# Attention: two-column minima and sums by one-source reductions instead of two-operand operations

## The chip, the cores and the metric

The kernel runs on one core of one Trainium2 chip. A core has TensorE (PE), VectorE (DVE), ScalarE (ACT), GpSimd (POOL) and a queue engine (SP), which run side by side and wait for each other by semaphores. The metric is the device time of one execution in microseconds, from the first to the last instruction of the program. Times are compared by the median of several executions.

## What is computed

A trunk of two layers over 1024 latent tokens and 256 context tokens in float32. The second layer's mixer is attention in two kinds of heads, 8 of each, with 64 columns: global heads that see all 1280 keys, and windowed heads that see the 256 context keys and three blocks of 128 latent keys and have one learned sink logit each. What matters here is the softmax:

```python
def attend(q, k, v, mask=None, sink=None):
    s = jnp.einsum('bqhgd,bkhd->bhgqk', q, k).astype(jnp.float32) * (HEAD_DIM ** -0.5)
    ...
    if sink is not None:
        col = jnp.broadcast_to(sink.astype(jnp.float32)[None, :, :, None, None], s.shape[:-1] + (1,))
        p = jax.nn.softmax(jnp.concatenate([s, col], axis=-1), axis=-1)[..., :-1]
    else:
        p = jax.nn.softmax(s, axis=-1)
    return jnp.einsum('bhgqk,bkhd->bqhgd', p.astype(v.dtype), v)
```

## The kernel before, in words

The attention is cut into 32 units: 2 kinds of heads, 2 groups of four heads, 8 blocks of 128 queries. The first 16 units are global (1280 keys, in ten blocks), the last 16 windowed with a sink (four or five blocks). The scores come negated, so that a row's greatest score is a minimum here, and the exponential is taken with a scale of −1.

For each head `h` of a unit `i`, TensorE writes the scores into PSUM: 1024 columns in `S` and 256 in `M` for a global head, one stretch of 512 or 640 columns in `S` for a windowed head (`do_chunk`, L2113). DVE takes the minimum of each part (`do_max`, L2119) into the tile `mx`, whose three rows of four columns hold the minimum of the first part, that of the second, and what is used. `do_bias` (L2125) takes the smaller of two columns: those of the two parts for a global head, that of the scores and the negated sink (`sinkn`) for a windowed head. ACT then takes the exponential with that column as its bias (`do_exp`, L2134) into `P` and adds up the row into a column of `rsum`, one for each part. In a windowed unit DVE adds the sink to the four minima (`do_arg`, L2140) and ACT takes the exponential of that as the second row of `rsum` (`do_sexp`).

After the four heads, TensorE transposes `P` by blocks of keys (`do_T`), ACT copies each block to `tf` (L2153), POOL rounds it to `th` (helper `rnd`, L73), and DVE, for the first block POOL, takes the rest `tl` = `tf` − `th` (helper `rest`, L77); TensorE multiplies `th` and `tl` with the values into `pv`. `do_recip` adds the two rows of `rsum` (L2179) and takes the reciprocal (L2180), POOL spreads it out to `R` (L2186), TensorE transposes it, ACT copies it. ACT copies parts of `pv` to `Yt` (L2206, L2207), DVE adds them into `Y` (L2213, L2214), POOL scales `Y` (L2219) and ACT and POOL split it into `ah` and `al`. In the first half, POOL also works on slices of the output weights (`woraw`, `woh`, `wol`, from `wo_steps`).

The order on all engines is made by a small planner at the end of `attention_units`: each step has an engine, a planned duration, a due time and the steps before it, and the steps are issued in the order in which the planner starts them. The planned durations are in the `op(...)` calls, and the engines carry their instructions out in that order.

Of the kernel before, what the change touches and what calls it, by code (L numbers as in the profile page):

```python
# [10 lines left out]
F32 = mybir.dt.float32  # L11
F32R = mybir.dt.float32r
AF = mybir.ActivationFunctionType
ALU = mybir.AluOpType
AX = mybir.AxisListType
# [22 lines left out]
def kernel(  # L38
# [6 lines left out]
    nc = tc.nc  # L45
    uid = [0]

    def nm(s):
        uid[0] += 1
        return f"{s}_{uid[0]}"  # L50
# [1994 lines left out]
    def attention_units(p, psS, psM, psT, psV, kv0, identr, bandr, sinkc, sinkn, wo_steps):  # L2045

        units = [(kind, g, qb) for kind in range(2) for g in range(2) for qb in range(8)]
# [3 lines left out]
        st, K, V = {}, {}, {}  # L2051
# [23 lines left out]
        def window(qb):  # L2075
            lo, hi = max(0, qb - 1), min(8, qb + 2)
            return 256 + lo * 128, (hi - lo) * 128
# [8 lines left out]
        def score_groups(i, h):  # L2086

            kind, g, qb = units[i]
            kh, kl = K[kind, g]
            q = st["q", i][:, h, :]  # L2090
            X = psS.tile([128, 1024], F32, tag="S", name=nm("S"))
            if not kind:
                M = psM.tile([128, 256], F32, tag="M", name=nm("M"))
                return ([(o, [(q, kh[:, k0:k0 + n]), (q, kl[:, k0:k0 + n])])
                         for o, k0, n in ((X[:, 0:512], 0, 512), (X[:, 512:1024], 512, 512), (M, 1024, 256))],
                        [X, M])
            k0, n = window(qb)
            b0 = 128 if qb == 0 else 0
            return ([(X[:, 256:512], [(q, kh[:, 0:256]), (q, kl[:, 0:256])]),
                     (X[:, 512:512 + n], [(q, kh[:, k0:k0 + n]), (identr, bandr[:, b0:b0 + n]), (q, kl[:, k0:k0 + n])])],  # L2100
                    [X[:, 256:512 + n]])

        def do_chunk(i, h, c):
            if c == 0:
                st["ch", i, h], st["sc", i, h] = score_groups(i, h)
            o, ops = st["ch", i, h][c]
            for x_, (l_, r_) in enumerate(ops):
                if l_ is identr and o.shape[1] == 384:

                    nc.tensor.matmul(o.rearrange("p (b k) -> p b k", k=128)[:, 0::2, :], lhsT=l_,  # L2110
                                     rhs=r_.rearrange("p (b k) -> p b k", k=128)[:, 0::2, :], start=False, stop=False)
                    continue
                nc.tensor.matmul(o, lhsT=l_, rhs=r_, start=x_ == 0, stop=x_ == len(ops) - 1)  # L2113


        def do_max(i, h, c):
            if h == 0 and c == 0:
                st["mx", i] = p.tile([128, 3, 4], F32, tag="mx", bufs=3, name=nm("mx"))
            nc.vector.tensor_reduce(out=st["mx", i][:, c, h:h + 1], in_=st["sc", i, h][c], axis=AX.X, op=ALU.min)  # L2119

        def do_bias(i, h):
            kind, g, qb = units[i]
            mx = st["mx", i]
            other = sinkn[:, 4 * g + h:4 * g + h + 1] if kind else mx[:, 1, h:h + 1]
            nc.vector.tensor_tensor(out=mx[:, 2, h:h + 1], in0=mx[:, 0, h:h + 1], in1=other, op=ALU.min)  # L2125

        def do_exp(i, h, c):
            if ("rs", i) not in st:
                st["rs", i] = p.tile([128, 2, 4], F32, tag="rsum", bufs=3, name=nm("rsum"))
            if ("P", i, h) not in st:  # L2130
                st["P", i, h] = p.tile([128, 1280], F32, tag=f"P{h}", bufs=2, name=nm("P"))
            rs, P, mx = st["rs", i], st["P", i, h], st["mx", i]
            o = st["sc", i, h][c]
            nc.scalar.activation(out=P[:, 1024 * c:1024 * c + o.shape[1]], in_=o, func=AF.Exp, scale=-1.0,  # L2134
                                 bias=mx[:, 2, h:h + 1], accum_out=rs[:, c, h:h + 1])
# [39 lines left out]

        def do_recip(i):
            rs3 = st.pop(("rs", i))
            rs = rs3[:, 0, :]
            nc.vector.tensor_tensor(out=rs, in0=rs, in1=rs3[:, 1, :], op=ALU.add)  # L2179
            nc.vector.reciprocal(out=rs, in_=rs)  # L2180
            st["rc", i] = rs

# [61 lines left out]
        for x_, (i, h) in enumerate(heads):  # L2244
            kind, n = units[i][0], nkb[i]
            t = starts[i] + h * (starts[i + 1] - starts[i]) / 4.0
            two = [("exp", *heads[x_ - 2], 0)] if x_ >= 2 else []
            one = [("exp", *heads[x_ - 1], 1)] if x_ >= 1 and not units[heads[x_ - 1][0]][0] else []
            width = 128 * (n - 2) + 256
            op(("chunk", i, h, 0), "PE", 0.215 if kind else 0.43, t, do_chunk, i, h, 0, deps=two)  # L2250
            op(("chunk", i, h, 1), "PE", (0.485 if n == 5 else 0.33) if kind else 0.43, t, do_chunk, i, h, 1,
               deps=[("chunk", i, h, 0)])
            if not kind:
                op(("chunk", i, h, 2), "PE", 0.215, t, do_chunk, i, h, 2, deps=[("chunk", i, h, 1)] + one)
            op(("max", i, h, 0), "DVE", 0.065 + width / 960.0 if kind else 1.131, t - 0.3, do_max, i, h, 0,
               deps=[("chunk", i, h, 1)])
            if not kind:
                op(("max", i, h, 1), "DVE", 0.333, t - 0.3, do_max, i, h, 1, deps=[("chunk", i, h, 2), ("max", i, h, 0)])
            op(("bias", i, h), "DVE", 0.075, t + 0.4, do_bias, i, h, deps=[("max", i, h, c) for c in range(2 - kind)])
            free_P = [("T", i - 2, nkb[i - 2] - 1)] if i >= 2 else []  # L2260
            op(("exp", i, h, 0), "ACT", 0.24 + width / 1200.0 if kind else 1.092, t + 2.7, do_exp, i, h, 0,
               deps=[("bias", i, h)] + free_P)
            if not kind:
                op(("exp", i, h, 1), "ACT", 0.452, t + 1.6, do_exp, i, h, 1, deps=[("bias", i, h)] + free_P)
# [18 lines left out]
            if kind:  # L2283
                op(("arg", i), "DVE", 0.08, T0, do_arg, i, deps=[("bias", i, h_) for h_ in range(4)])
                op(("sexp", i), "ACT", 0.19, T0 + 0.5, do_sexp, i, deps=[("arg", i)] + exps)
                exps.append(("sexp", i))
            op(("recip", i), "DVE", 0.30, T0 + 1.0, do_recip, i, deps=exps)
            op(("R", i), "Pool", 0.37, T0 + 1.0, do_R, i, deps=[("recip", i), ("RT", i - 1)])
            op(("RT", i), "PE", 0.22, T0 + 1.9, do_RT, i, deps=[("R", i), ("T", i, 0)], take="T")
# [55 lines left out]
        for x_, k in enumerate(order):  # L2345
            i = k[1]
# [483 lines left out]
```

## Time and profile before

| | us |
|---|---|
| median of three runs (2981.91 to 2985.57) | 2983.54 |
| the profiled execution | 2980.23 |
| its span from first to last instruction | 2978.5 |
| attention, global units (1786 to 2049 us of the span) | 263 |
| attention, windowed units (2049 to 2206 us) | 157 |
| TensorE busy over the span | 2793.1 (94%) |
| DVE busy over the span | 2138.9 (72%) |
| POOL busy over the span | 663.0 (22%) |

Busy shares over the whole span are means over stages that are limited by different engines; the edited lines run only in the attention, so its two halves are looked at by themselves. An operation's duration in the profile reaches from its start on the engine to its end and includes time in which it can't go on.

### The profile page before, as it was taken

The page shows a single profiled execution, that of the slowest core. Times are in us where ns is not written, and L with a number is a line of the kernel's source. Part 1 is how long each engine was busy: PE and PEld are TensorE (multiplying, and loading weights), DVE is VectorE, ACT ScalarE, POOL GpSimd, SP SyncE. Part 2 cuts the span into 40 slices and gives each one's busy share as a digit, 9 for nine tenths or more (in the row PEclk, how much of TensorE's full clock was granted, in tenths as well). Part 3 has the DMA queues.
Part 4 walks back from the last instruction along what each step waited for, and adds up shares of the span by engine and source line. Part 5 has one row for each costly group of instructions (what it writes and reads, how often), then busy time and mean ns, then how long its engine had stood idle before and what let it go on. Part 6 is the DMA issues. An engine that isn't in the chain of part 4 may idle for free. (4 is left out here: it accounts for less than half of the span.)

```text
span 2978.5 us, 37852 instructions
## 1 busy us (share of the span) xinstructions
PE 2793.1 (94%) x13912; PEld 2260.6 (76%) x13912; DVE 2138.9 (72%) x2995; ACT 1281.4 (43%) x2229; POOL 663.0 (22%) x729
## 2 busy tenths in 40 slices
PE   7999999887899999999999989998889899999997
PEld 4777767665688888888877876666768688888886
DVE  4898943545766666666776668999884877886778
ACT  2555531345322222234364527777764422222433
POOL 5223313111000000000024345777751000000002
PEclk9999999999899999999999999999999999999998
DMA  6344445665133355475675562102012343454854
GB/s 223 123 153 152 138 141 176 197 176 146 59 90 91 91 159 157 157 254 185 191 207 140 176 207 57 40 27 56 29 45 98 95 125 109 154 177 157 297 170 121
DMA packets 310809, 412.78 MB, mean 139 GB/s; under 512 B 19888, under 2 KB 188680, under 8 KB 305504
## 3 DMA queue, kind: packets, MB, share of 16 engines
q1 hardware_dynamic: 296608, 387.24, 41.0%
q0 software_dynamic: 8640, 15.79, 3.2%
q10 hardware_dynamic: 5376, 7.34, 0.7%
q8 instruction: 109, 1.79, 0.3%
q14 instruction: 76, 0.62, 0.1%
HBM read 311.85 MB, written 98.45 MB: 138 GB/s over the span
## 5 line engine op out<-in xcount | busy, mean ns | idle before, releaser
L80 PE MATMUL fi<-ah,sop 128*128 128x512 f32 (+1 forms) x1056 | 379.2, 359 | 16.3 <-ACT sop L69 13.3
L82 PE MATMUL fi<-ah,sop 128*128 128x512 f32 (+1 forms) x1056 | 377.6, 358 | 0.6 <-DVE sop L77 0.5
L81 PE MATMUL fi<-al,sop 128*128 128x512 f32 (+1 forms) x1056 | 377.8, 358 | 0.3 <-DVE al L77 0.3
L69 ACT CAST sop<-sraw 128x1024 fp32r<-128x1024 f32 (+1 forms) x198 | 176.5, 901 | 264.9 <-DVE sraw L1125 195.1
L77 DVE TENSOR_TENSOR sop<-sraw,sop 128x1024 fp32r<-128x1024 f32 (+1 forms) x198 | 203.8, 1047 | 93.6 <-ACT sop L69 93.6
L80 PEld LDWEIGHTS fi<-ah,sop 128*128 128x128 f32 x1056 | 202.7, 192 | 45.5 <-ACT sop L69 14.1
L82 PEld LDWEIGHTS fi<-ah,sop 128*128 128x128 f32 x1056 | 201.8, 191 | 30.9 <-DVE sop L77 2.6
L81 PEld LDWEIGHTS fi<-al,sop 128*128 128x128 f32 x1056 | 202.3, 192 | 28.7 <-DVE al L77 0.8
L80 PE MATMUL fi<-T,sop 128*128 128x512 f32 x528 | 206.6, 391 | 8.8 <-ACT T L69 7.2
L82 PE MATMUL fi<-T,sop 128*128 128x512 f32 x528 | 206.2, 391 | 0.5 <-DVE sop L77 0.5
L81 PE MATMUL fi<-T,sop 128*128 128x512 f32 x528 | 206.4, 391 | 0.0
L73 POOL TENSOR_SCALAR th<-tf 128x512 fp32r<-128x512 f32 x236 | 163.8, 706 | 97.6 <-ACT tf L2153 93.8
L77 DVE TENSOR_TENSOR tl<-tf,th 128x512 fp32r<-128x512 f32 x204 | 171.9, 857 | 13.1 <-POOL th L73 12.4
L80 PE MATMUL ip<-ah,whi 128*128 128x512 f32 (+1 forms) x480 | 175.6, 366 | 3.6 <-ACT ah L69 3.5
L81 PE MATMUL ip<-al,whi 128*128 128x512 f32 (+1 forms) x480 | 171.7, 358 | 0.5 <-DVE al L77 0.4
L82 PE MATMUL ip<-ah,wlo 128*128 128x512 f32 (+1 forms) x480 | 170.7, 356 | 0.0
L80 PE MATMUL fo<-fow,fos 128*128 128x512 f32 x385 | 150.6, 391 | 3.5 <-DVE acc L1128 2.2
L2153 ACT COPY tf<-T 128x512 f32<-128x512 f32 x236 | 133.3, 592 | 41.1 <-PE T L2148 25.5
L82 PE MATMUL fo<-fow,fos 128*128 128x512 f32 x385 | 150.0, 390 | 0.1
L81 PE MATMUL fo<-fow,fos 128*128 128x512 f32 x385 | 149.9, 389 | 0.0
L2148 PE MATMUL T<-ident,P 128*128 128x128 f32 x944 | 139.7, 274 | 1.4 <-ACT tf L2153 0.4
L2119 DVE TENSOR_REDUCE mx<-S 128x1 f32<-128x1024 f32 (+2 forms) x128 | 127.8, 999 | 14.2 <-PE S L2113 13.0
(413 smaller groups left out, 7092.5 us busy)
## 6 DMA issues: line engine op xcount, KB each, us to landing
sraw<-in_ffn_w_in_dram SPq DMA_DIRECT2D x88, 512.0 KB
adaraw<-in_ada_w_dram SPq DMA_DIRECT2D x40, 1024.0 KB
stream<-sd_d SPq DMA_DIRECT2D x77, 320.0 KB
stream<-in_ffn_w_out_dram SPq DMA_DIRECT2D x78, 256.0 KB
wt<-sd_d SPq DMA_DIRECT2D x77, 256.0 KB
sd_d<-hp SPq DMA_DIRECT2D x22, 640.0 KB
wt<-in_ffn_w_out_dram SPq DMA_DIRECT2D x55, 256.0 KB
h_d<-acc SPq DMA_DIRECT2D x26, 512.0 KB
```

The source lines that it names most:

```text
L69: nc.scalar.copy(out=o, in_=i)
L73: nc.gpsimd.tensor_scalar(out=o, in0=i, scalar1=1.0, scalar2=0.0, op0=ALU.mult, op1=ALU.add)
L77: e.tensor_tensor(out=o, in0=i, in1=hi.bitcast(F32), op=ALU.subtract)
L80: nc.tensor.matmul(ps, lhsT=sh, rhs=mh, start=start, stop=False)
L81: nc.tensor.matmul(ps, lhsT=sh, rhs=ml, start=False, stop=False)
L82: nc.tensor.matmul(ps, lhsT=sl, rhs=mh, start=False, stop=stop_)
L2119: nc.vector.tensor_reduce(out=st["mx", i][:, c, h:h + 1], in_=st["sc", i, h][c], axis=AX.X, op=ALU.min)
L2148: nc.tensor.transpose(ps_[:, x_ * 128:(x_ + 1) * 128], st["P", i, h][:, j * 128:(j + 1) * 128], ident)
L2153: nc.scalar.copy(out=tf, in_=st.pop(("T", i, j)))
```

## The change

The minimum of two columns and the sum of two rows, which were tensor_tensor operations, become tensor_reduce operations over an axis of two elements of one tile. For that, both values have to stand in one tile. In global units they do. In windowed units POOL first copies the four negated sinks of the group into the second row of `mx`, one new POOL operation a unit; so `mx` is taken in `do_chunk`, ahead of the unit's first scores, and no longer in `do_max`. `do_arg` later writes over that row, as before. `rsum` gets a third row for the sum, which was written in place.

```diff
--- before.py
+++ after.py
@@ -2103,6 +2103,12 @@
         def do_chunk(i, h, c):
             if c == 0:
                 st["ch", i, h], st["sc", i, h] = score_groups(i, h)
+            if h == 0 and c == 0:
+                st["mx", i] = p.tile([128, 3, 4], F32, tag="mx", bufs=3, name=nm("mx"))
+                kind, g = units[i][:2]
+                if kind:
+                    nc.gpsimd.tensor_scalar(out=st["mx", i][:, 1, :], in0=sinkn[:, 4 * g:4 * g + 4], scalar1=1.0, scalar2=0.0,
+                                            op0=ALU.mult, op1=ALU.add)
             o, ops = st["ch", i, h][c]
             for x_, (l_, r_) in enumerate(ops):
                 if l_ is identr and o.shape[1] == 384:
@@ -2114,19 +2120,15 @@
 
 
         def do_max(i, h, c):
-            if h == 0 and c == 0:
-                st["mx", i] = p.tile([128, 3, 4], F32, tag="mx", bufs=3, name=nm("mx"))
             nc.vector.tensor_reduce(out=st["mx", i][:, c, h:h + 1], in_=st["sc", i, h][c], axis=AX.X, op=ALU.min)
 
         def do_bias(i, h):
-            kind, g, qb = units[i]
             mx = st["mx", i]
-            other = sinkn[:, 4 * g + h:4 * g + h + 1] if kind else mx[:, 1, h:h + 1]
-            nc.vector.tensor_tensor(out=mx[:, 2, h:h + 1], in0=mx[:, 0, h:h + 1], in1=other, op=ALU.min)
+            nc.vector.tensor_reduce(out=mx[:, 2, h:h + 1], in_=mx[:, 0:2, h], axis=AX.X, op=ALU.min)
 
         def do_exp(i, h, c):
             if ("rs", i) not in st:
-                st["rs", i] = p.tile([128, 2, 4], F32, tag="rsum", bufs=3, name=nm("rsum"))
+                st["rs", i] = p.tile([128, 3, 4], F32, tag="rsum", bufs=3, name=nm("rsum"))
             if ("P", i, h) not in st:
                 st["P", i, h] = p.tile([128, 1280], F32, tag=f"P{h}", bufs=2, name=nm("P"))
             rs, P, mx = st["rs", i], st["P", i, h], st["mx", i]
@@ -2175,8 +2177,8 @@
 
         def do_recip(i):
             rs3 = st.pop(("rs", i))
-            rs = rs3[:, 0, :]
-            nc.vector.tensor_tensor(out=rs, in0=rs, in1=rs3[:, 1, :], op=ALU.add)
+            rs = rs3[:, 2, :]
+            nc.vector.tensor_reduce(out=rs, in_=rs3[:, 0:2, :].rearrange("p c h -> p h c"), axis=AX.X, op=ALU.add)
             nc.vector.reciprocal(out=rs, in_=rs)
             st["rc", i] = rs
 
```

On DVE a piece of a global unit's instructions stood so before the change (`mx` the minima, `tl` the rest of a block, `rsum` the row sums, `Y` the output of the unit before; the number behind a name tells buffers apart):

```order
L2119 TENSOR_REDUCE mx_15908<-M_15870 128x1
L2179 TENSOR_TENSOR rsum_15737<-rsum_15737 128x4
L2180 RECIPROCAL rsum_15737<-rsum_15737 128x4
L2125 TENSOR_TENSOR mx_15908<-mx_15908 128x1
L77 TENSOR_TENSOR tl_15948<-tf_15914,th_15929 128x512
L77 TENSOR_TENSOR tl_15957<-tf_15927,th_15936 128x512
L2119 TENSOR_REDUCE mx_15908<-S_15923 128x1
L2119 TENSOR_REDUCE mx_15908<-M_15924 128x1
L2125 TENSOR_TENSOR mx_15908<-mx_15908 128x1
L2213 TENSOR_TENSOR Y_16001<-pv_15807,Yt_15983 64x256
```

And so after it:

```order
L2123 TENSOR_REDUCE mx_15871<-M_15870 128x1
L2181 TENSOR_REDUCE rsum_15737<-rsum_15737 128x4
L2182 RECIPROCAL rsum_15737<-rsum_15737 128x4
L2127 TENSOR_REDUCE mx_15871<-mx_15871 128x1
L77 TENSOR_TENSOR tl_15948<-tf_15914,th_15929 128x512
L77 TENSOR_TENSOR tl_15957<-tf_15927,th_15936 128x512
L2123 TENSOR_REDUCE mx_15871<-S_15923 128x1
L2123 TENSOR_REDUCE mx_15871<-M_15924 128x1
L2127 TENSOR_REDUCE mx_15871<-mx_15871 128x1
L2215 TENSOR_TENSOR Y_16001<-pv_15807,Yt_15983 64x256
```

No instruction of DVE has moved; three lines of the piece have another operation and one source less. On PE, ACT and SP the order is the same too.

On POOL a piece of the windowed units stood so (`th` the rounded block, `al` the second part of the output's split, `R` the spread reciprocals):

```order
L73 TENSOR_SCALAR th_17908<-tf_17893 128x512
L77 TENSOR_TENSOR al_1842_13924<-Y_17865,ah_1841_13923 128x2x128
L2186 TENSOR_SCALAR R_17944<-rsum_17804 128x256
L73 TENSOR_SCALAR th_17971<-tf_17961 128x512
L2219 TENSOR_TENSOR Y_17963<-Y_17963,rT_17861 128x256
L77 TENSOR_TENSOR tl_17986<-tf_17961,th_17971 128x512
L73 TENSOR_SCALAR th_18008<-tf_17980 128x512
```

And after the change so:

```order
L73 TENSOR_SCALAR th_17915<-tf_17898 128x512
L77 TENSOR_TENSOR al_1842_13924<-Y_17870,ah_1841_13923 128x2x128
L2188 TENSOR_SCALAR R_17950<-rsum_17809 128x256
L73 TENSOR_SCALAR th_17977<-tf_17967 128x512
L2221 TENSOR_TENSOR Y_17969<-Y_17969,rT_17866 128x256
L77 TENSOR_TENSOR tl_17992<-tf_17967,th_17977 128x512
L2110 TENSOR_SCALAR mx_18009<-sinkn 128x4
L73 TENSOR_SCALAR th_18016<-tf_17986 128x512
```

The copy of the sinks (L2110) has been put between `tl` and `th`; there are 16 such copies, one a windowed unit, and nothing else on POOL has moved.

## Rows read from the trace of the kernel before

**Rows 1.** Windows: the two halves of the attention; busy us and instructions by engine, granted clock.

```profile
core 0: us, PE busy (x) PEld busy (x) DVE busy (x) ACT busy (x) POOL busy (x), PEclk, DMA share, GB/s
1786.00:2049.00 263.00, 238.50 (x1302) 177.52 (x1302) 245.37 (x385) 199.20 (x460) 179.46 (x224) 0.99 0.17 44
2049.00:2206.00 157.00, 139.35 (x848) 111.67 (x846) 143.00 (x276) 119.87 (x295) 111.49 (x147) 0.99 0.13 35
```

**Rows 2.** Chain that ended last, over 1870 to 1954 us: its shares by line.

```profile
by line: DVE tl L77 33.2%; DVE mx L2119 26.3%; DVE mx L2125 6.2%; POOL th L73 5.0%; PE T L2148 3.7%; PE S L2113 3.6%; issue 2.9%; PE pv L2174 2.8%; DVE Y L2214 2.0%; DVE Y L2213 1.9%; POOL wol L77 1.7%; PE pv L2173 1.7%; POOL woraw L2371 1.
```

**Rows 3.** Groups by line and form, DVE, 1786 to 2210 us (busy us, mean ns of one).

```profile
L77 DVE TENSOR_TENSOR tl<-tf,th 128x512 fp32r<-128x512 f32 x202 | 170.0, 855 | 13.1 <-POOL th L73 12.4
...
L2125 DVE TENSOR_TENSOR mx<-mx 128x1 f32<-128x1 f32 x64 | 28.3, 443 | 1.1
...
L2125 DVE TENSOR_TENSOR mx<-mx,sinkn 128x1 f32<-128x1 f32 x64 | 25.3, 396 | 0.8
...
L2179 DVE TENSOR_TENSOR rsum<-rsum 128x4 f32<-128x4 f32 x32 | 7.2, 225 | 0.0
...
L2140 DVE TENSOR_TENSOR mx<-mx,sinkc 128x4 f32<-128x4 f32 x16 | 7.2, 450 | 0.4
```

**Rows 4.** Line L2125: durations in ns (shortest, median, longest); who waited (us, times).

```profile
L2125 DVE TENSOR_TENSOR mx<-mx x64: 128/452/1232, 1786.6 to 2047.7; 128x1 f32<-128x1 f32 x64
...
L2125 DVE TENSOR_TENSOR mx<-mx,sinkn x64: 128/324/1244, 2049.4 to 2203.1; 128x1 f32<-128x1 f32 x64
...
  ACT P L2134: 45.1, 55
```

**Rows 5.** Timeline of DVE, 1943 to 1951.3 us (start us, duration us).

```profile
1943.78 0.56 DVE L2125 TENSOR_TENSOR mx<-mx 128x1 f32<-128x1 f32 x1
...
1944.26 0.68 DVE L77 TENSOR_TENSOR tl<-tf,th 128x512 fp32r<-128x512 f32 x1
...
1947.35 0.45 DVE L2125 TENSOR_TENSOR mx<-mx 128x1 f32<-128x1 f32 x1
...
1947.72 1.48 DVE L77 TENSOR_TENSOR tl<-tf,th 128x512 fp32r<-128x512 f32 x2
...
1950.70 0.56 DVE L2125 TENSOR_TENSOR mx<-mx 128x1 f32<-128x1 f32 x1
...
1951.27 0.42 DVE L2213 TENSOR_TENSOR Y<-pv,Yt 64x256 f32<-64x256 f32 x1
```

**Rows 6.** Timeline of POOL, 1943 to 1952 us.

```profile
1943.60 0.73 POOL L73 TENSOR_SCALAR th<-tf 128x512 fp32r<-128x512 f32 x1 [0.28 <-ACT tf L2153]
...
1946.60 1.20 POOL L73 TENSOR_SCALAR th<-tf 128x512 fp32r<-128x512 f32 x2 [2.26 <-ACT tf L2153]
...
1950.05 1.20 POOL L73 TENSOR_SCALAR th<-tf 128x512 fp32r<-128x512 f32 x2 [1.39 <-ACT tf L2153]
```

**Rows 7.** Groups by line and form, POOL, 1786 to 2210 us.

```profile
L2371 POOL TENSOR_TENSOR woraw<-woraw,wogate 128x512 f32<-128x512 f32 x6 | 9.5, 1579 | 0.0
```

**Rows 8.** DVE operations with one source in SBUF: shortest, median, longest in ns.

```profile
L2180 DVE RECIPROCAL rsum<-rsum x32: 177/178/180, 1796.7 to 2206.3; 128x4 f32<-128x4 f32 x32
...
L1866 DVE TENSOR_REDUCE ss<-t x13: 404/674/685, 1594.0 to 1742.9; 128x8 f32<-128x512 f32 x8, 128x4 f32<-128x256 f32 x5
```

**Rows 9.** Groups by form of line L1866 on DVE (busy us, mean ns of one).

```profile
L1866 DVE TENSOR_REDUCE ss<-t 128x8 f32<-128x512 f32 x8 | 5.4, 678 | 2.0 <-ACT t L1863 2.0
...
L1866 DVE TENSOR_REDUCE ss<-t 128x4 f32<-128x256 f32 x5 | 2.1, 413 | 1.6 <-ACT t L1863 1.6
```

**Rows 10.** Timeline of ACT, 1943.5 to 1951.9 us; idle time before in brackets.

```profile
1947.84 0.47 ACT L2134 ACTIVATE P<-M,mx 128x256 f32<-128x256 f32 x1 [0.84 <-DVE mx L2125]
...
1950.87 0.36 ACT L2207 COPY Yt<-pv 64x256 f32<-64x256 f32 x1
```

**Rows 11.** Timeline of DVE in the second half, 2110 to 2125 us.

```profile
2116.84 0.56 DVE L2125 TENSOR_TENSOR mx<-mx,sinkn 128x1 f32<-128x1 f32 x1
...
2118.08 0.82 DVE L2119 TENSOR_REDUCE mx<-S 128x1 f32<-128x640 f32 x1 [0.40 <-PE S L2113]
```

**Rows 12.** POOL tensor_scalar of line L129: shortest, median, longest in ns.

```profile
L129 POOL TENSOR_SCALAR rs<-mv x46: 212/222/1240, 442.7 to 2969.1; 128x1 f32<-128x1 f32 x46
```

## The prediction

> **What bounds the kernel now.** Read first the busy time of each engine over the attention, the only part in which the edited lines run. VectorE (DVE) is busy 245.4 of 263 us in the first half (the global heads) and 143.0 of 157 us in the second (the windowed heads with a sink), TensorE 238.5 and 139.4, GpSimd (POOL) 179.5 and 111.5 [rows 1]. Then the chain of work that ended last, over a stretch of the first half: the two largest entries are DVE's subtractions `tl` (L77, 33.2%) and its score minima (L2119, 26.3%), the third is L2125, one of the two edited lines, with 6.2% [rows 2]. So DVE sets the pace here. A one-column minimum has no business among the first three, which makes its duration the next thing to look at.
>
> L2125 takes one column from each of two sources, and yet its mean is 443 ns in the first half and 396 ns in the second [rows 3]; its shortest case is 128 ns, its longest 1244 [rows 4]. What fills the rest is seen in time. In one unit of the first half the minimum that starts at 1943.78 lasts 0.56 us, until 1944.34; POOL's rounding `th` that started at 1943.60 ends at 1944.33. The one at 1947.35 and the one at 1950.70 likewise end at 1947.80 and 1951.26, and POOL's pairs of `th` end at 1947.80 and 1951.25 [rows 5, 6]. An operation of DVE with two sources in SBUF thus waits until POOL's running operation is over. Operations of DVE with one source don't: RECIPROCAL on the same row sums has 177 to 180 ns in all 32 cases, and the tensor_reduce of L1866, which also reads float32 from SBUF, between 404 and 685 ns over its two widths, whose means are 413 and 678 ns [rows 8, 9].
>
> **The change part by part.** *Price of the new operation.* No row has a tensor_reduce over two columns. From the two widths of L1866, (678 − 413) / 256 = 1.04 ns a column, so a fixed part of 413 − 256 × 1.04 = 147 ns, and two columns cost about 149 ns. From above, RECIPROCAL's 178 ns bounds it; from below, the shortest minimum of today, 128 ns. I take 149. Eight columns for the row sums come to 155 ns.
>
> The Trainium skill speaks against the swap: VectorE: DVE Perf Modes, section "Rules for kernel authors", says of tensor_reduce on a hot path that it is the slowest DVE operation and should be restructured. At two columns the price above differs from the uncontended minimum by some 20 ns; by that rule alone the 160 swaps would cost 3 us, and nothing would come back.
>
> *Most that can come off.* 64 minima cost 28.3 us in the first half, 64 cost 25.3 in the second, the 32 sums of row sums 7.2 [rows 3]. New: 128 × 0.149 + 32 × 0.155 = 24.0 us. So 60.8 − 24.0 = 36.8 us of DVE time is the waiting in these lines, and the end of the range if all of it were worth its time.
>
> *Where the wait goes.* Most is not removed but handed on. In the first listing of the order one minimum is followed on DVE by a subtraction `tl` and one by `Y`; over a whole unit of the first half it is three and one. `tl` has two SBUF sources and waits for POOL by itself: mean 855 ns against the 0.68 us of the row at 1944.26 [rows 3, 5]. With the minimum done at 1943.93, `tl` is next in line and still can't begin before POOL's `th` ends at 1944.33; it began at 1944.26. The same at 1947.35: the pair of `th` ends at 1947.80 and the `tl` pair began at 1947.72. What such a minimum saves on DVE is its own short turn after the wait, which I put at 0.05 us (the 0.08 us by which `tl` could start sooner on paper, less what POOL takes back).
>
> What does come free is the result. ScalarE (ACT) stands 45.1 us in 55 waits for this minimum before an exponential [rows 4]; at 1947.84 it had been idle 0.84 us [rows 10]. There the bias comes (0.45 − 0.15) = 0.3 us earlier by itself and, with what is gained at 1943.78, about 0.5. ACT then runs its exponentials and copies that much ahead, so the `Yt` copies, which end at 1951.23, come earlier too. That matters at the third minimum: 1950.70 to 1951.26, after it `Y` at 1951.27, which needs `Yt` [rows 5, 10]. Today both hold `Y`; after the change the minimum ends at 1950.85 and `Yt` lies before that. So here 0.56 − 0.15 = 0.41 us falls out of DVE's line with nothing behind it that waits. A unit of the first half (263 / 16 = 16.4 us) then gains 0.41 + 2 × 0.05 = 0.5 us. Six times in this half POOL also works on a slice of the output weights, beginning with 1.6 us at L2371 [rows 7]; in six of the 16 units it is longer in the way, and there I take half. First half: 10 × 0.5 + 6 × 0.25 = 6.5 us.
>
> Second half: 25.3 − 64 × 0.149 = 15.8 us of waiting, 1.0 us in a unit of 157 / 16 = 9.8. Here more of the next operations want no second source, but the last minimum of a unit is followed by L2140, which has two sources (450 ns mean [rows 3]) and inherits the wait, and after another, at 2116.84, DVE stands idle 0.40 us for the scores of TensorE [rows 11]. I keep a third: 5.3 us.
>
> *What is added.* 16 POOL operations on 4 columns, one a unit in the second half. The nearest row, a tensor_scalar of POOL on one column, has a median of 222 ns and a maximum of 1240 [rows 12]. 16 × 0.22 = 3.5 us; POOL is idle 45 of 157 us [rows 1], so half of it lands on something that waits: 1.7 us. In POOL's order it stands with a `th`, an `al` or a `Y` right behind it, which it delays (the second listing). DVE's first minimum of the unit comes only after the unit's first scores, so I put nothing on that wait. The tile `mx` is now taken with the scores and not with their minimum; three are in rotation, and the one reused is three units old.
>
> GPSIMD Engine Reference and SBUF — State Buffer (section "SBUF: two separate sides") of the Trainium skill say that a POOL operation that reads SBUF holds the port pair it shares with DVE for its whole length. By that rule each of the 16 is also a new thing for `tl` to wait for, and all of the 3.5 us would count, not half; the gain would be 8.3 us in place of the sum below.
>
> *Sum.* 6.5 + 5.3 − 1.7 = 10.1 us. I assume, without a row for it, that what follows the attention starts that much earlier and the gain reaches the end. The profiled execution took 2980.2 us (span 2978.5); it becomes 2970. The median of the three runs shown lies 3.3 us above the profiled one, so the forecast is 2983.5 − 10.1 = 2973.4 us.
>
> **Rivals.** *The wait is handed on whole.* Every minimum that loses its wait is followed by a `tl` or L2140 that takes it over, and ACT's earlier start only makes `th` earlier, into another `tl`. For it: `tl` already waits 0.18 us in the mean and most minima stand ahead of one. Against it: `Y` and the score minima behind L2125 have no second SBUF source. Then 0 to 6 us come off: 2978 to 2984, 2981 in the middle.
>
> *Most of it counts.* DVE is busy 93% of the first half and ACT's 45.1 us are on the way to the next copies; if the earlier exponentials pull POOL ahead so that DVE finds it idle, 25 of the 36.8 us come off: 2958. Against it: TensorE is busy 91% and would be the next bound.
>
> *POOL's new operation delays the second half.* The place is `th`, which POOL does one after another and for which `tl` and so TensorE wait. If each of the 16 waits for the port as long as the longest of [rows 12], 1.24 us, and all of that is on the path, it costs 19.8 us against 11.8 gained: 2991.5. It turns the sign from 11.8 / 16 = 0.74 us each. Against it: the median is 222 ns, and POOL idles 28% of this half.
>
> *The change doesn't do what it says.* If a two-column tensor_reduce also waited for POOL, all times would stay: 2983. The single-source rows speak against it [rows 8].
>
> **How the numbers follow.** The measurement of this kernel can tell about 0.2%, 6 us, from no change. Chances: the forecast 0.52 (its own range 2966 to 2977), most of it counts 0.13, handed on whole 0.24, no effect at all 0.03, POOL's delay 0.08. Faster by over 6 us: 0.52 + 0.13, with a little of the middle case, 0.66; within: 0.26; slower: 0.08. The range goes from 2959, which cuts off half of "most of it counts", to 2983, which leaves out the slower case and the upper end of the handed-on one.
>
> **What would show each step.** Right: the minima near 150 ns with hardly any spread, no case over 250; their sum near 19 us in place of 53.6; `tl`'s mean higher than 855 ns, since it takes over part of the wait; ACT's wait for the minimum well under 45 us; the first half shorter by about 6 us, the second by 3 to 4. Wrong: minima still up to 0.5 us or more; `tl` up by as much as the minima fell (202 × 0.15 us would eat 30 us); new idle time on DVE before L2123 or on POOL behind the copy of the sink; or an attention that is shorter while the end is not.

## The result, and the profile after

The changed kernel takes 2967.41 us (median of five, 2967.03 to 2971.84), the kernel before 2982.61 us (2981.82 to 2985.57) in its five: a ratio of 0.9949 with a 95% interval of 0.9938 to 0.9960, so 12 to 18 us faster; the medians differ by 15.2 us. The forecast was 10.1 us. The profiled execution's span went from 2978.5 to 2965.5 us.

Where it came from is read best as the length of the attention: from the start of the first score matmul (writing `S`) to the start of the first matmul of the output projection (`oo`), both from the groups of those tiles. Before: 1780.7 to 2217.7 us, 436.9 us. After: 1782.7 to 2205.1 us, 422.3 us (lengths are taken before rounding), or 14.6 less. What follows it is as long as it was in these two executions (760.8 and 760.4 us), so the whole gain of the attention reaches the end in them; the 2 us by which it begins later belong to the work ahead of it, which the change doesn't touch.

The groups of DVE in the changed kernel by line and form, over 1776 to 2210 us (busy us, mean ns of one), answer to [rows 3]:

```profile
L77 DVE TENSOR_TENSOR tl<-tf,th 128x512 fp32r<-128x512 f32 x204 | 187.5, 934 | 17.4 <-POOL th L73 16.5
...
L2127 DVE TENSOR_REDUCE mx<-mx 128x1 f32<-128x2 f32 x128 | 18.7, 146 | 1.9
...
L2142 DVE TENSOR_TENSOR mx<-mx,sinkc 128x4 f32<-128x4 f32 x16 | 7.0, 436 | 0.4
...
L2181 DVE TENSOR_REDUCE rsum<-rsum 128x4 f32<-128x8 f32 x32 | 4.7, 147 | 0.0
```

The 128 minima went from 28.3 + 25.3 to 18.7 us, the 32 sums from 7.2 to 4.7: 37.4 us of DVE's time are gone. The subtraction `tl`, whose own work is the same, went from 855 to 934 ns: 204 × 0.079 = 16.1 us have come back in it. L2140 of before, the addition of the sink (here L2142), did not take over more of the wait: 450 ns before, 436 now. The line of the minima by itself (shortest, median, longest in ns, then who waited for it, us and times) answers to [rows 4]:

```profile
L2127 DVE TENSOR_REDUCE mx<-mx x128: 123/146/157, 1788.6 to 2190.9; 128x1 f32<-128x2 f32 x128
...
  ACT P L2136: 27.9, 48
```

Not one of the 128 waits any more, and ACT's wait for them fell from 45.1 to 27.9 us. In the chain that ended last, over the stretch of the changed kernel that answers to [rows 2] (1868 to 1952 us), the line of the minima is no longer among the entries shown, and entries of ACT and POOL have moved up:

```profile
by line: DVE tl L77 30.3%; DVE mx L2123 23.4%; ACT P L2136 6.9%; issue 6.4%; POOL th L73 5.9%; ACT tf L2155 5.9%; POOL woraw L2373 3.5%; POOL woh L73 2.3%; DVE Y L2216 2.0%; DVE Y L2215 1.9%; ACT Yt L2209 1.8%; ACT Yt L2208 1.8%; POOL wol L
```

The same unit as in [rows 5], in the timeline of DVE of the changed kernel (start us, duration us):

```profile
1945.34 0.18 DVE L2182 RECIPROCAL rsum<-rsum 128x4 f32<-128x4 f32 x1
1945.44 0.12 DVE L2127 TENSOR_REDUCE mx<-mx 128x1 f32<-128x2 f32 x1
1945.48 1.83 DVE L77 TENSOR_TENSOR tl<-tf,th 128x512 fp32r<-128x512 f32 x2
...
1948.81 0.15 DVE L2127 TENSOR_REDUCE mx<-mx 128x1 f32<-128x2 f32 x1
1949.02 0.42 DVE L2215 TENSOR_TENSOR Y<-pv,Yt 64x256 f32<-64x256 f32 x1
...
1960.91 0.18 DVE L2182 RECIPROCAL rsum<-rsum 128x4 f32<-128x4 f32 x1
```

And ACT in the same unit (idle time before in brackets), which answers to [rows 10]:

```profile
1945.60 0.48 ACT L2136 ACTIVATE P<-M,mx 128x256 f32<-128x256 f32 x1 [0.57 <-DVE mx L2127]
...
1948.63 0.36 ACT L2209 COPY Yt<-pv 64x256 f32<-64x256 f32 x1
```

Both kinds of place are seen, a minimum ahead of a `tl` and one ahead of `Y`. From the start of the minimum of 1945.44 to the end of the two `tl` behind it are 1.87 us; before they were 1947.72 + 1.48 − 1947.35 = 1.85 [rows 5]. That minimum no longer waits, and the pair waits that much longer, 1.83 us in place of 1.48. From the start of the minimum of 1948.81 to `Y` are 0.21 us; before they were 1951.27 − 1950.70 = 0.57. Here 0.36 us are gone for good. What `Y` also needs came sooner by nearly as much: ACT begins its exponential 1945.60 − 1945.44 = 0.16 us after the start of the first of these two minima, where it was 1947.84 − 1947.35 = 0.49, and works without a gap until `Yt` is done at 1948.99. The minimum ahead of `Y` is over at 1948.96. So `Y`, at 1949.02, starts when both are done, as it did before. From one reciprocal to the next the unit has 1960.91 − 1945.34 = 15.57 us; it had 16.09 (1947.26 to 1963.35 in the same timeline before).

The copies of the sinks, which had no row before, answer to [rows 12]; the row gives shortest, median and longest of POOL's line in ns:

```profile
L2110 POOL TENSOR_SCALAR mx<-sinkn x16: 189/203/638, 2041.6 to 2183.8; 128x4 f32<-128x4 f32 x16
```

### The profile page after: what moved, and what is told of

It is laid out like the page before. It is cut to its first block, busy times and chain, and to the rows that moved or that the text cites. A ratio compares the mean times of both kernels' runs of the same rounds, so it can differ in the third digit from the quotient of the medians.

```text
span 2965.5 us, 37868 instructions
## 1 busy us (share of the span) xinstructions
PE 2787.8 (94%) x13912; PEld 2262.2 (76%) x13912; DVE 2119.1 (71%) x2995; ACT 1282.3 (43%) x2229; POOL 674.8 (23%) x745
## 5 line engine op out<-in xcount | busy, mean ns | idle before, releaser
L77 DVE TENSOR_TENSOR tl<-tf,th 128x512 fp32r<-128x512 f32 x204 | 187.5, 934 | 17.4 <-POOL th L73 16.5
L73 POOL TENSOR_SCALAR th<-tf 128x512 fp32r<-128x512 f32 x236 | 174.3, 749 | 79.5 <-ACT tf L2155 78.4
L81 PE MATMUL fo<-fow,fos 128*128 128x512 f32 x385 | 150.4, 391 | 0.0
```

What stands on the lines that cost most here:

```text
L73: nc.gpsimd.tensor_scalar(out=o, in0=i, scalar1=1.0, scalar2=0.0, op0=ALU.mult, op1=ALU.add)
L77: e.tensor_tensor(out=o, in0=i, in1=hi.bitcast(F32), op=ALU.subtract)
L81: nc.tensor.matmul(ps, lhsT=sh, rhs=ml, start=False, stop=False)
```

## The experiments

**What to compare.** The times of the whole kernel scatter by several us on some of the chips used, more than most of these differences. The length of the attention scatters less, which one more profiled execution of each kernel shows.

> The kernel before once more, for its trace alone: what the length of the attention varies by from one execution to the next. If units fall into other phases by chance, single units differ by 0.5 to 1 us and the halves (253.6 and 156.1 us) by 1 to 3; if the phase is set by the program, they repeat within 0.3 us.

> The changed kernel once more, for its trace alone: the halves of the attention (247.3 and 147.6 us) repeat within 0.3 us if the program sets them, or vary by 1 to 3 us if units fall into other phases by chance.

Before, again: 437.3 us (436.9 the first time); after, again: 423.1 (422.3). Single units repeat within 0.2 us, but for two in the changed kernel that are 0.5 us off. One of these, the eleventh, has 17.9 us at a granted clock of TensorE of 1.00 of full speed the first time, and 18.4 us at 0.91 the second. So one kernel repeats within 1 us.

Different kernels with the same code in one half do not always agree that well. The second half repeats: 156.1 to 156.2 us in the three executions with the code of before, 147.6 and 148.1 in the changed kernel. The first half has 253.6, 253.8 and 255.8 us with the code of before, and 247.3 to 249.1 us in six executions with the code of the changed kernel; the longest of each have more time at the lower of the two levels of TensorE's granted clock, 1.2 and 2.4 GHz (0.99 of full speed in the mean against 1.00, and 0.97 against 0.99). A difference of the first half under some 2 us can't be put down to an edit by itself.

In the table the halves go from the first `rsum` reciprocal to the sixteenth, and from there to the last (before: 1796.68, 2050.27 and 2206.34 us); the times are those of the profiled execution, the clock is the granted one of its first half as a share of full speed, the ratio that of the timed runs to the kernel before on the same chip, with its 95% interval.

| kernel | attention us | first half | its clock | second half | ratio |
|---|---|---|---|---|---|
| before | 436.9 | 253.6 | 1.00 | 156.1 | 1 |
| changed | 422.3 | 247.3 | 0.99 | 147.6 | 0.9949 (0.9938 to 0.9960) |
| sums alone | 435.9 | 253.2 | 0.98 | 155.8 | 0.9989 (0.9981 to 0.9998) |
| global minima alone | 433.8 | 250.6 | 0.98 | 156.1 | 0.9983 (0.9974 to 0.9992) |
| windowed minima and copies alone | 432.2 | 255.8 | 0.99 | 150.4 | 0.9985 (0.9974 to 0.9995) |
| global minima and sums | 431.4 | 249.1 | 0.97 | 156.1 | 0.9969 (0.9958 to 0.9979) |
| both minima, sums as before | 426.8 | 249.9 | 0.99 | 149.8 | 0.9960 (0.9946 to 0.9973) |
| changed, three copies a unit | 426.5 | 247.5 | 0.99 | 152.6 | 0.9968 (0.9956 to 0.9980) |
| changed, sinks copied once | 422.9 | 248.0 | 0.99 | 148.6 | 0.9951 (0.9939 to 0.9963) |
| the same, sink added by reduction | 423.1 | 248.1 | 0.99 | 147.6 | 0.9952 (0.9939 to 0.9965) |
| minimum by per-row scalar | 427.9 | 250.5 | 0.98 | 150.0 | 0.9970 (0.9958 to 0.9981) |
| the same, sums by reduction | 424.2 | 249.1 | 0.98 | 148.3 | 0.9955 (0.9942 to 0.9968) |

**One part alone.** The three parts of the change were run each by itself. The edit for the global minima, with sums and windowed minima as before and no copies:

```diff
+            if kind:
+                nc.vector.tensor_tensor(out=mx[:, 2, h:h + 1], in0=mx[:, 0, h:h + 1], in1=sinkn[:, 4 * g + h:4 * g + h + 1], op=ALU.min)
+            else:
+                nc.vector.tensor_reduce(out=mx[:, 2, h:h + 1], in_=mx[:, 0:2, h], axis=AX.X, op=ALU.min)
```

> Only the 64 minima of the global units are reductions; the windowed minima and the sums of row sums stay two-operand, and there is no copy of the sinks. Theory (each half pays for itself, and what comes free is the bias that ACT and Y wait for): the first half is shorter by about 6 us, the second the same, 2976.5 us in all. Rival (the earlier POOL work of one half only shifts the wait, so the parts don't add): under 3 us, 2980 or more.

Measured: 2976.51 us, first half 3.0 us shorter, second unchanged. The mechanism holds, half of the size is missing; one unit of this half is 1.0 us longer than before, at the lower clock level (the last heading).

> Only the 64 minima of the windowed units are reductions, with the 16 copies of the sinks on POOL; global minima and sums stay two-operand. The prediction's term for this half: 5.3 - 1.7 = 3.6 us, 2979 us in all. The theory after the result (about two thirds of the waiting of this half comes free): 8 us in the second half, 2974.5 us in all, first half unchanged.

Measured: 2977.67 us, second half 5.7 us shorter, between the two readings. (The first half is 2.2 us longer in this execution, in units whose code is that of before. Two units are 0.85 us longer each, and each stands right behind a unit at a granted clock of 0.90 or 0.91, where the kernel before has 1.00. That the clock is the cause is likely and was not tried.)

> Only the 32 sums of two row sums are reductions; both kinds of minima stay two-operand, no copies. Theory: 2.2 us of waiting in all, nearly all of it ahead of a minimum that waits in its place: within 1 us of before, 2982 us. Rival: the sums unlock the reciprocal and POOL's R for each unit: 2 us or more off, 2980.

Measured: 2979.08 us, attention 1.0 us shorter. The three parts alone give 3.1 + 4.7 + 1.0 = 8.8 us, the whole change 14.6. In the first half that doesn't show by itself that the parts help each other: all three had more time at the lower clock level there than the kernel before. In the second half, which repeats, the parts alone give 5.7 + 0.3 = 6.0 us and the whole change 8.4 (8.0 in the second execution). There the parts do help each other, and the next runs asked which.

**Both minima without the sums.**

```diff
-            rs = rs3[:, 2, :]
-            nc.vector.tensor_reduce(out=rs, in_=rs3[:, 0:2, :].rearrange("p c h -> p h c"), axis=AX.X, op=ALU.add)
+            rs = rs3[:, 0, :]
+            nc.vector.tensor_tensor(out=rs, in0=rs, in1=rs3[:, 1, :], op=ALU.add)
```

> The changed kernel with the sums of row sums put back to two-operand form: both kinds of minima are reductions, the copies of the sinks stay. From the first sum's reciprocal to the last the trace showed 409.7 us before, 394.9 after, 406.7 with the global minima alone, 406.1 with the windowed ones alone, 409.0 with the sums alone. If the parts add, this kernel has 409.7 - 3.0 - 3.6 = 403 us (2975 us in all). If the sums take over the wait that the minima give up, so that only both together pay: also 401 to 403. If the sums don't matter and the odd phases of single units made the parts look small: 395 to 397 us (2968 in all).

Measured: 2970.03 us, attention 426.8, first to last reciprocal 249.9 + 149.8 = 399.7 us: between the readings. Reducing the sums as well is worth 426.8 − 422.3 = 4.5 us here (3.7 by the second execution of the changed kernel), where alone it was worth 1.0; 1.3 us of that go with the clock in one unit (the last heading). In the second half it is 149.8 − 147.6 = 2.2 us (1.7), against 0.3 alone. The groups of DVE show why (busy us, mean ns). The line of the sums in this kernel in the second half:

```profile
L2181 DVE TENSOR_TENSOR rsum<-rsum 128x4 f32<-128x4 f32 x16 | 5.7, 353 | 0.0
```

And in the second half of the kernel before:

```profile
L2179 DVE TENSOR_TENSOR rsum<-rsum 128x4 f32<-128x4 f32 x16 | 2.8, 174 | 0.0
```

With the minima no longer waiting, the two-operand sum waits more, 309 ns in the mean of all 32 in place of 225 [rows 3]. All of that comes from the second half, 353 ns in place of 174; in the first it is 264 in place of 276. With the windowed minima alone it is 353 ns there too, with the per-row scalar 271. Why an operation of POOL runs at that moment more often now wasn't traced. The sum stands ahead of the reciprocal and of a minimum, and so of what ACT and POOL wait for. Reducing it hands nothing on to `tl`, which has 932 ns here and 934 in the changed kernel.

**Global minima and sums, windowed part as before.**

> Global minima and all sums are reductions; the windowed minima stay two-operand and there are no copies. First half (first to sixteenth reciprocal): 247.3 us as in the changed kernel if the sums pay there together with the minima, 250.6 if not. Second half: 156 us as before if the sums alone do nothing there, about 153 if they pay by themselves. In all 2975 us with the first reading, 2978 with the second.

Measured: 2974.72 us, first half 249.1 us, between the readings; second half 156.1, so sums alone do nothing there. The first half is 1.5 us shorter than with the global minima alone, but the unit of the last heading has 1.4 us of that, and over the other units nothing is left. So this pair doesn't show that the sums pay in the first half. Two of its units are 0.7 and 0.9 us longer than in the changed kernel, both in or right behind a stretch at the lower clock level (granted clock 0.91 and 0.92 in the eleventh and the fourth unit, 1.00 in the changed kernel).

**The price of the copies.** Three in place of one, then six in all in place of 16:

```diff
-                if kind:
+                for _ in range(3 * kind):
                     nc.gpsimd.tensor_scalar(out=st["mx", i][:, 1, :], in0=sinkn[:, 4 * g:4 * g + 4], scalar1=1.0, scalar2=0.0,
```

> The changed kernel with three copies of the sinks in a row on POOL a windowed unit in place of one (32 more, each some 0.2 us by itself and 0.39 us in the mean with its waits). If all of a copy is on the path: 32 x 0.2 = 6.5 us or more, 2974 us or later. If half of it is, as the prediction put it: 3.3 us, 2970.6 us. If POOL's idle time hides the copies: 2967.4 us, as the changed kernel.

Measured: 2972.92 us, attention 3.4 to 4.1 us longer than in the two executions of the changed kernel: 0.11 to 0.13 us a copy, a third of what one lasts with its waits in the changed kernel (389 ns in the mean).

```diff
+        def sink_mx(g, r):
+            if ("smx", g, r) not in st:
+                t = st["smx", g, r] = p.tile([128, 4, 4], F32, name=nm("smx"))
+                nc.gpsimd.tensor_scalar(out=t[:, 1, :], in0=sinkn[:, 4 * g:4 * g + 4], scalar1=1.0, scalar2=0.0,
+                                        op0=ALU.mult, op1=ALU.add)
+            return st["smx", g, r]
...
+                    st["mx", i] = sink_mx(g, i % 3)
```

> The changed kernel, but the windowed units use six lasting tiles (three for each group of heads) into which POOL copies the sinks once each, and the sum of minimum and sink goes to a fourth row: 6 copies in place of 16. If half of each copy is on the path: 10 x 0.39 / 2 = 2 us less than the changed kernel, 2965.5 us. If all: 4 us, 2963.5. If none: 2967.4 us.

Measured: 2966.98 us, attention 422.9: no difference from 422.3 and 423.1. Ten copies fewer give nothing, 32 more cost some 4 us. So one copy a unit seems to find time on POOL in which nothing waits for it, and further ones only in part; which operations wait for them wasn't worked out.

**The last two-operand addition as well.** The sink is added to the four minima by a reduction over two rows of the lasting tile:

```diff
-            nc.vector.tensor_tensor(out=mx[:, 3, :], in0=mx[:, 2, :], in1=sinkc[:, 4 * g:4 * g + 4], op=ALU.add)
+            nc.vector.tensor_reduce(out=mx[:, 4, :], in_=mx[:, 2:4, :].rearrange("p c h -> p h c"), axis=AX.X, op=ALU.add)
```

> As the kernel with lasting tiles, and the 16 additions of the sink to the four minima, which still have two sources and last 436 ns in the mean, become reductions over two rows as well (the sinks themselves stand in a further row). Theory (what follows decides): 16 x (436 - 150) = 4.6 us of waiting, of which the share that the windowed minima kept, some 60%, comes off: 2 to 3 us below the kernel with lasting tiles. Rival (the next subtraction takes it over): no difference.

Measured: 2969.68 us, attention 423.1. The addition fell from 390 ns in the mean to 157, 3.7 us over the 16, and no gain shows in the attention: the rival. Of the 3.7 us, 1.8 stand in `tl` (187.9 to 189.7 us); the second half is 1.0 us shorter, but what stands between the last reciprocal and the output projection is 1.3 us longer. So about half was seen to be taken over, and the rest is not accounted for.

**A second value that is not a second tensor.**

```diff
-            nc.vector.tensor_tensor(out=mx[:, 2, h:h + 1], in0=mx[:, 0, h:h + 1], in1=other, op=ALU.min)
+            nc.vector.tensor_scalar(out=mx[:, 2, h:h + 1], in0=mx[:, 0, h:h + 1], scalar1=other, scalar2=None, op0=ALU.min)
```

> The kernel before with one edit: the minimum is a tensor_scalar whose source is one column and whose per-row scalar is the other column (min), for both kinds of heads; no copies, sums as before. Theory A (it is the second source as such, from wherever an operation takes it, or a float32 tensor_scalar that reads through both ports, as the one of L2021 that lasted 694 ns for 8 columns): minima still spread up to 0.5 us and over, time as before, 2982.6 us. Theory B (a per-row scalar doesn't count, one column reads by one port): minima near 150 ns, and without copies 2 us below the changed kernel, 2965.5 us.

Measured: 2972.45 us. The line by itself (shortest, median, longest in ns), in the global and in the windowed units:

```profile
L2125 DVE TENSOR_SCALAR mx<-mx x64: 182/212/216, 1783.8 to 2042.4; 128x1 f32<-128x1 f32 x64
L2125 DVE TENSOR_SCALAR mx<-mx,sinkn x64: 183/203/216, 2043.7 to 2191.5; 128x1 f32<-128x1 f32 x64
```

None waits, so theory B: both values still come from SBUF, and it is the second tensor operand that waits for POOL, not the second value. The time is that of the kernel with both minima and unchanged sums (427.9 and 426.8 us), not 2965.5 us; the sums may be what was missing. With them:

> The kernel with the minimum as a tensor_scalar over one column (its minima lasted 182 to 216 ns and none waited), and with the sums as reductions; no copies of the sinks. If the sums were what that kernel lacked: first half 247 us, second 147 to 148, 2967 us in all, as the changed kernel. If its minima, 60 ns longer than the reductions, were: no change from 250.5 and 150.0 us, 2972 in all. A version that beats the changed kernel would need under 2966.

Measured: 2970.14 us, attention 424.2: the sums give 1.4 us in the first half, at the same granted clock, and 1.6 in the second. It does without the copies and comes near the changed kernel, but does not beat it; its first half is 1.6 to 1.8 us longer, of which one unit alone has 1.3 to 1.5 (the last heading). No version that was run is faster than the changed kernel beyond the scatter.

## Why the prediction was right

**The price** was right: 146 ns for two columns (149 forecast), 147 for eight (155), against means of 443, 396 and 225 before. The loss of 3 us that the prediction worked out from the rule of the Trainium skill (VectorE: DVE Perf Modes, section "Rules for kernel authors") did not come: the swaps took 14.6 us off the attention.

**The waits go on to `tl`**: right. Of the 37.4 us that the edited lines lost, 16.1 stand in `tl` now. L2140, which was to inherit the wait in the second half, did not. The rival in which all is handed on would have given 0 to 6 us, the one in which most counts 25; the attention gave 14.6. That is less than the 37.4 − 16.1 = 21.3 us because DVE stands idle more: of its 409.7 us from the first to the last reciprocal 27.0 were idle, and 33.4 of 394.9 are now. The rival in which the change does nothing falls by the minima, none of which has over 157 ns.

**ACT's earlier start** was right in kind: its wait for the minimum fell by 17.2 us, and the unit looked at is 0.52 us shorter, where 0.5 was forecast: 0.36 us ahead of `Y` (forecast 0.41), nothing at the `tl` pair (0.05), and 0.16 in the rest of the unit. The forecast let `Yt` come 0.5 us sooner and so lie ahead of the minimum; it came 0.33 sooner against ACT's work ahead of it, and is done 0.03 us behind the minimum. That ACT's start is what lets `Y` begin sooner was read from the rows and not tried by itself.

**First half**: 6.5 forecast, 6.3 measured, and that they meet so closely is in part luck. The minima without the sums give 3.0 to 3.7 us, or 4.3 to 5.0 without the 1.3 that go with the clock in one unit. The prediction has no term for the clock, and it put the sums at nothing: their waiting, 7.2 − 32 × 0.155 = 2.2 us, is inside the 36.8, with no term of their own. At one and the same granted clock, in the kernels with a per-row scalar, the sums give 1.4 us in this half, though kernels with the same code there differ by as much.

**Second half**: the term 5.3 − 1.7 = 3.6 us was mis-sized; it measured 8.4. Three things are in it. The minima with the copies paid gave 5.7 to 6.2 us, 36 to 39% of the 15.8, so "I keep a third" was near for them. The copies were put at 1.7 us; 16 at the price of an extra one would be 1.7 to 2.1, but taking ten away gave nothing. And the sums, put at nothing, gave the rest: 2.2 us (1.7 by the second execution) with the minima reduced, 0.3 alone. Here the step that failed is the one that let the wait go to `tl` and L2140 only: it went to the sums too, 353 ns in place of 174, and taking it from them as well paid.

**POOL's delay**, the slower rival, needed 0.74 us a copy. An extra copy cost 0.11 to 0.13 us, and the longest of the 16 has 638 ns.

**After the attention** the gain passed whole in the first pair of executions, as assumed: 760.8 and 760.4 us to the end. In the second it was 760.3 and 763.1; TensorE was busy there for 732.4 us in place of 730.2. The 15.2 us between the medians of the timed runs say that the gain reaches the end on the whole.

The Trainium skill (SBUF — State Buffer, section "SBUF: two separate sides") says that DVE and POOL share a pair of ports, that an operation of DVE takes part when it has two SBUF inputs (against a POOL operation that reads SBUF) or runs in a mode that uses both ports, and that whoever starts first keeps it for the whole operation. The minima agree: 128 to 1244 ns with two tensor operands, 123 to 157 with one. What the runs add is that a per-row scalar from SBUF doesn't count as the second input: 182 to 216 ns. By the price that the prediction worked out from this rule, all 3.5 us of the copies would count; an extra copy cost 0.11 to 0.13 us, 1.7 to 2.1 for 16. Of the two pages of the Trainium skill that the prediction names for it, this is the one that states how long the ports are held.

The prediction's sentence that operations of DVE with one source don't wait is too wide. L2021, a one-source tensor_scalar over 8 columns that runs once, lasted from 1798.70 to 1799.39 us in the kernel before, and POOL's `tl` from 1798.10 to 1799.37; in the changed kernel it ended at 1801.35 and POOL's `tl` at 1801.33. In all executions together it lasted 634 to 925 ns; the one-column tensor_scalar lasted 217 at most. So how many sources an operation has doesn't settle by itself whether it waits; in which mode it ran can't be seen in the trace.

## What to carry to other kernels

A tiny operation whose durations spread from 0.13 to 1.2 us, as here, is waiting and not working for most of them; look for what the other engine is doing at its end, and for a form with one tensor operand (a reduction over two neighbours, a per-row scalar on one column). Such a wait moves to the next operation of the same kind, so try all of them that stand close together on the path, the cheap-looking ones too (the sums paid, the addition of the sink didn't), and price the gain by what stands behind each and not by the time they lose. When single units are compared, compare their granted clock first.

## What the runs showed that was not expected

One unit of the first half, with a slice of the output weights on POOL, takes 18.6 us in the changed kernel and 19.9 to 20.0 us in four of the experiments (global minima alone, both minima, and the two with a per-row scalar). In the kernel with both minima and the sums as before, TensorE stood idle twice ahead of it, as its timeline shows (idle time in brackets):

```profile
2000.92 0.50 PE L2175 MATMUL pv<-th,va 128*128 128x512 f32 x1 [1.66 <-POOL th L73]
2002.04 0.79 PE L2176 MATMUL pv<-tl,va 128*128 128x512 f32 x1 [0.62 <-DVE tl L77]
```

From there its granted clock was at the lower of its two levels, 1.2 GHz, for 6 us, though it was busy without a break. Busy time in that unit by stretches, and the granted clock (PEclk), in the same kernel:

```profile
core 0: us, PE busy (x) PEld busy (x) DVE busy (x) ACT busy (x) POOL busy (x), PEclk, DMA share, GB/s
1991.05:2002.05 11.00, 8.69 (x51) 6.16 (x49) 8.10 (x15) 8.00 (x20) 9.70 (x12) 0.97 0.01 1
2002.05:2005.05 3.00, 3.00 (x10) 2.26 (x11) 3.00 (x4) 1.19 (x3) 2.13 (x3) 0.50 0.00 0
2005.05:2008.05 3.00, 3.00 (x11) 2.41 (x11) 1.49 (x4) 1.64 (x5) 1.01 (x2) 0.50 0.52 175
```

And of the changed kernel, at the same place of the unit:

```profile
1994.36:2005.36 11.00, 8.70 (x50) 6.22 (x48) 8.17 (x15) 7.97 (x20) 9.79 (x13) 1.00 0.00 0
2005.36:2008.36 3.00, 2.96 (x10) 2.14 (x10) 3.00 (x4) 1.21 (x3) 2.16 (x3) 0.53 0.03 5
2008.36:2011.36 3.00, 3.00 (x19) 2.49 (x17) 2.21 (x5) 2.20 (x5) 1.33 (x2) 0.90 0.52 175
```

The same work, nearly the same stretch ahead of it, and the clock comes back some 2.5 us sooner. The unit is 1.3 us longer, so about that much of the difference between these kernels goes with when the clock rises and not with the time of the edited lines; what moves that moment wasn't tried. In the kernel before it doesn't fall in that unit at all, and the unit takes 18.9 us.
